# Weights' buffers at the far end of SBUF, every later tile 52 KB lower

## The chip, the cores and the metric

The kernel runs on one core of one Trainium2 chip. The metric is the device time of one execution in microseconds; lower is better. Three runs of the kernel before gave 2146.89, 2148.67 and 2943.94 us; the median, 2148.67 us, is the time before. The profile is of one further execution, which took 2149.47 us.

## The reference

Two decoder layers over a residual stream x of 512 tokens and 1024 channels, in float32. Each layer has three parts: a half-step SwiGLU feed-forward network (FFN) of width 2816, a token mixing of 16 heads in three groups, and a second half-step FFN. Shift, scale and gate of every part come from silu(c) times a matrix.

```python
def swiglu(h, w1, w3, w2):
    return (jax.nn.silu(h @ w1) * (h @ w3)) @ w2
...
        h = modulate(rmsnorm(x, norm_g[layer, 0]), sh1, sc1)
        x = x + 0.5 * g1 * swiglu(h, ffn_w1[layer, 0], ffn_w3[layer, 0], ffn_w2[layer, 0])

        h = modulate(rmsnorm(x, norm_g[layer, 1]), sh2, sc2)
        proj = h @ w_in[layer]
...
        o = jnp.concatenate([oa, ob, oc], axis=2)
        o = (_rms(o).reshape(B, S, D_MIX) * out_g[layer].astype(jnp.float32)).astype(x.dtype)
        x = x + g2 * (o @ w_out[layer])

        h = modulate(rmsnorm(x, norm_g[layer, 2]), sh3, sc3)
        x = x + 0.5 * g3 * swiglu(h, ffn_w1[layer, 1], ffn_w3[layer, 1], ffn_w2[layer, 1])
```

## The kernel before

**Layout of the data.** x lies transposed in SBUF, eight tiles of 128 channels by 512 tokens. All matrices are read from HBM in 338 pieces of at most 128 x 1024 float32 (512 KB), in the order of use. `fetch` (L262) loads a piece into a tile `raw` by a DMA on the SP queue and copies it on ScalarE to `whi` in the type float32r; `load_piece` (L273) lets VectorE write the rest, `wlo` = `raw` - `whi` (L280). Activations are split the same way: normalized x into `hh` and `hl`, the FFN's gated product into `gh` and `gl`.

**The product.** Every large product is done in three matmuls, `mm3` (L302): high by high (L308), high by low (L309), low by high (L310). A matmul on TensorE has a stationary operand (at most 128 x 128, brought in by a weight load that the profile lists as PEld) and a moving operand that streams past it.

- In the first half of an FFN (`h @ w1`, `h @ w3`) a slice of 128 columns of `whi` or `wlo` is stationary and `hh` or `hl` moves, 512 columns at a time.
- In the second half (`@ w2`) a slice of `whi` or `wlo` is stationary and `gh` or `gl` moves, 512 columns; the last two outputs of each FFN are done in halves of 256 columns (`TAIL`, `HALVES`). The first head of the next FFN and the output projection (`out_last`) also move `hh` and `hl` 256 columns at a time.
- In the mixing, `proj_tok` (L542) has it the other way round: `hh` or `hl` is stationary and `whi` or `wlo` moves, 256 or 328 columns. `proj_feat` (L557) has weights stationary and `hh` or `hl` moving, 512 columns, in bursts of 24 matmuls.

TensorE therefore reads two SBUF tiles at a time: the moving one, and the stationary one of the next matmul.

**The order.** Within an engine instructions run in program order. The mixing's order over its parts is written out by hand (`PLAN`, L130). There are three `raw` buffers and five each of `whi` and `wlo`, so that loading, splitting and multiplying overlap: ScalarE's copy of a piece waits until TensorE has done with the piece five before.

**Where the tiles lie.** Each pool is a stretch of every partition; pools are laid one behind the other in the order in which they are opened in `Net.__init__` and later, and tiles keep fixed addresses. Counting the tiles' sizes gives this map (bytes from the start of a partition; the last column is the address modulo 512, the size of a row of 128 float32 numbers):

| pool and tile | address | modulo 512 |
|---|---|---|
| `consts`: x and the small tables; `rmat` at 19,520 | 1,152 to 24,128 | 64 (`rmat`) |
| `weights`: 3 `raw`, 5 `whi`, 5 `wlo`, 4 KB each, 53,248 bytes in all | 24,128 to 77,376 | 64 |
| `acts`: 8 `hh`, 8 `hl`, 2 KB each | 77,376 to 110,144 | 64 |
| `tiny` | 110,144 to 113,600 | mixed |
| `fp` (open in the FFNs): `gh` and `gl` among them, 2 KB each | 125,888 to 195,520 | 448 |
| `mp` (open in the mixing): `qk`, `v`, `att` among them | 113,600 to 229,056 | 64 (these three) |

The FFNs' pool `fp` and the mixing's pool `mp` take turns in the stretch above 113,600.

Of the kernel before, what the change touches and what calls it, by code (L numbers as in the profile page):

```python
# [182 lines left out]
class Net:  # L183
    def __init__(self, tc, ctx, io):
        self.tc, self.nc, self.ctx, self.io = tc, tc.nc, ctx, io
        self.n = 0
        self.cp = ctx.enter_context(tc.tile_pool(name="consts", bufs=1))
        self.wp = ctx.enter_context(tc.tile_pool(name="weights", bufs=1))
        self.hp = ctx.enter_context(tc.tile_pool(name="acts", bufs=1))
        self.sp = ctx.enter_context(tc.tile_pool(name="tiny", bufs=1))  # L190
        pp = ctx.enter_context(tc.tile_pool(name="psum", bufs=1, space=PSUM))
        self.bank = lambda tag, shape: self.t(pp, tag, shape, bufs=2)
        self.new_z = lambda: self.t(pp, "z", [P, 1024], bufs=3)
        self.xs = self.cp.tile([P, KC, S], F32, name="xs")
        self.x = [self.xs[:, k, :] for k in range(KC)]
        self.piece, self.fetched = -1, None
        self.queue, self.delayed = [], []
        self.order = ExitStack()
# [951 lines left out]
```

## Time and profile before

| | |
|---|---|
| median of the three runs | 2148.67 us |
| the profiled execution | 2149.47 us |
| its span, first to last instruction | 2147.7 us |
| mean granted TensorE clock | 0.996 |
| busy: TensorE matmul / weight load / VectorE / ScalarE | 2094.9 / 1806.0 / 1305.2 / 831.2 us |
| read from HBM | 256.55 MB |

[...] In a view by stretches the count in brackets holds every instruction that runs at any time in the stretch, so also the ones still running at its left edge.

### The profile page before, as it was taken

To read this page: it belongs to the slowest core of one execution; us is meant where nothing else is said; L and a number is where in the kernel's file an instruction comes from. 1 tells how busy PE (TensorE), PEld (TensorE's weight loads), DVE (VectorE), ACT (ScalarE), POOL (GpSimd) and SP (SyncE) were. 2 spreads that over 40 slices of the span, in tenths; PEclk is the share of its full clock that TensorE was granted. 3 is DMA by queue.
4 is the path that set the end of the run, shared out by engine and by line. 5 is a ranking of instruction groups with operands and counts; after the bars stand their busy time and mean duration, and the time that the engine had idled before them with its cause. 6 is when DMAs were issued, how large, how long until landed. Compare 5 with 4: busy or idle time off the path is not lost.

```text
span 2147.7 us, 28762 instructions
## 1 busy us (share of the span) xinstructions
PE 2094.9 (98%) x11280; PEld 1806.0 (84%) x11280; DVE 1305.2 (61%) x2607; ACT 831.2 (39%) x1295; POOL 2.9 (0%) x12
## 2 busy tenths in 40 slices
PE   6999999999999999999999999999999999999999
PEld 5888888888998888888898888888889988888888
DVE  8772753679989777375364333346899886333332
ACT  3321222467664432122242222324766644222220
POOL 0000000000000000000000000000000000000000
PEclk9999999999999999999999999999999999999999
DMA  8783752342333378376334333324333223323331
GB/s 296 265 283 98 264 172 90 102 106 63 101 93 90 120 264 283 99 264 199 96 99 137 98 95 94 96 85 122 90 86 103 71 74 108 97 89 98 99 101 56
DMA packets 86151, 281.75 MB, mean 131 GB/s; under 512 B 10752, under 2 KB 13312, under 8 KB 86016
## 3 DMA queue, kind: packets, MB, share of 16 engines
q1 hardware_dynamic: 84576, 277.83, 41.5%
q8 instruction: 88, 1.44, 0.3%
q10 hardware_dynamic: 1440, 2.10, 0.3%
q14 instruction: 47, 0.39, 0.1%
HBM read 256.55 MB, written 2.10 MB: 120 GB/s over the span
## 4 chain that ended last, share of the span: by engine, by line
PE 82%; DVE 12%; ACT 2%; DMA 2%; issue 1%; SPq 0%; ACTq 0%; DVEq 0%
PE z L308 23%; PE z L310 23%; PE z L309 23%; PE b L308 3%; PE b L310 3%; PE b L309 3%; DVE att L568 2%; DVE sc L855 2%; DVE wlo L280 2%; DVE m L854 1%; PE z L613 1%; DMA qk<-qk 1%; PE z L657 1%; PE z L706 1%; DVE tf L718 1%
## 5 line engine op out<-in xcount | busy, mean ns | idle before, releaser
L280 DVE TENSOR_TENSOR wlo<-raw,whi 128x1024 fp32r<-128x1024 f32 (+1 forms) x338 | 412.2, 1220 | 537.4 <-ACT whi L270 535.2
L270 ACT CAST whi<-raw 128x1024 fp32r<-128x1024 f32 (+1 forms) x338 | 354.3, 1049 | 864.0 <-PE z L309 793.0
L308 PE MATMUL z<-hh,whi 128*128 128x512 f32 (+1 forms) x1616 | 597.1, 370 | 6.7 <-DVE xs L987 3.9
L310 PE MATMUL z<-hh,wlo 128*128 128x512 f32 (+1 forms) x1616 | 595.6, 369 | 1.9 <-DVE wlo L280 1.9
L309 PE MATMUL z<-hl,whi 128*128 128x512 f32 (+1 forms) x1616 | 596.8, 370 | 0.5
L308 PEld LDWEIGHTS z<-hh,whi 128*128 128x128 f32 x1616 | 305.7, 189 | 58.7 <-DVE xs L987 4.3
L310 PEld LDWEIGHTS z<-hh,wlo 128*128 128x128 f32 x1616 | 305.3, 189 | 53.2 <-DVE wlo L280 2.6
L309 PEld LDWEIGHTS z<-hl,whi 128*128 128x128 f32 x1616 | 305.7, 189 | 52.2 <-DVE hl L430 1.3
L308 PE MATMUL z<-gh,whi 128*128 128x512 f32 (+1 forms) x792 | 293.6, 371 | 0.0
L309 PE MATMUL z<-gl,whi 128*128 128x512 f32 (+1 forms) x792 | 292.7, 370 | 0.0
L310 PE MATMUL z<-gh,wlo 128*128 128x512 f32 (+1 forms) x792 | 289.3, 370 | 0.0
L349 DVE CUSTOM_DVE_ANT_0 adaw<-adaw,silc 128x1024 f32<-128x1024 f32 x144 | 171.0, 1221 | 26.2 <-DMA adaw<-in_w_ada_dram 26.1
L308 PEld LDWEIGHTS z<-gh,whi 128*128 128x128 f32 x792 | 148.9, 188 | 29.7
L310 PEld LDWEIGHTS z<-gh,wlo 128*128 128x128 f32 x792 | 148.9, 188 | 27.8
L309 PEld LDWEIGHTS z<-gl,whi 128*128 128x128 f32 x792 | 149.0, 188 | 26.6
L308 PE MATMUL b<-whi,hh 128*128 128x256 f32 x544 | 157.8, 290 | 4.1 <-DVE v L647 3.6
L310 PE MATMUL b<-whi,hl 128*128 128x256 f32 x544 | 155.7, 286 | 0.0
L309 PE MATMUL b<-wlo,hh 128*128 128x256 f32 x544 | 155.6, 286 | 0.0
L506 DVE SCALAR_TENSOR_TENSOR xs<-z,mod,xs 128x512 f32<-128x512 f32 (+1 forms) x72 | 49.7, 691 | 124.6 <-PE z L310 124.5
L308 PEld LDWEIGHTS b<-whi,hh 128*128 128x128 f32 x544 | 105.7, 194 | 5.1 <-issue 4.0
L309 PEld LDWEIGHTS b<-wlo,hh 128*128 128x128 f32 x544 | 105.7, 194 | 0.2
L310 PEld LDWEIGHTS b<-whi,hl 128*128 128x128 f32 x544 | 105.6, 194 | 0.0
(144 smaller groups left out, 2260.1 us busy)
## 6 DMA issues: line engine op xcount, KB each, us to landing
raw<-in_w_dram SPq DMA_DIRECT2D x332, 512.0 KB, 3.6
adaw<-in_w_ada_dram SPq DMA_DIRECT2D x144, 512.0 KB, 4.7
qk<-qk SPq DMA_DIRECT2D x144, 128.0 KB, 2.3
qk<-qk SPq DMA_DIRECT2D x24, 96.0 KB, 3.2
xs<-in_x_dram SPq DMA_DIRECT2D x4, 512.0 KB, 5.3
raw<-in_w_dram SPq DMA_DIRECT2D x4, 492.0 KB, 3.5
silc<-in_c_dram SPq DMA_DIRECT2D x3, 512.0 KB, 5.0
out_dram<-xs ACTq DMA_DIRECT2D x6, 256.0 KB, 2.0
```

The costliest lines, as they stand in the source:

```text
L270: nc.scalar.copy(hi[:, :n], raw[:, :n])
L280: self.nc.vector.tensor_sub(lo[:, :n], raw[:, :n], hi.bitcast(F32)[:, :n])
L308: mm(out, l[0], r[0], start=start, stop=False, **kw)
L309: mm(out, l[0], r[1], start=False, stop=False, **kw)
L310: mm(out, l[1], r[0], start=False, stop=stop, **kw)
L349: r = self.nc.vector.tensor_tensor_reduce(w, w, self.silc, 1.0, 0.0, op0=ALU.mult, op1=ALU.add, accum_out=m[:, j:j + 1])
L506: nc.vector.scalar_tensor_tensor(self.x[m][:, cs], ps[:, cs], gate[:, m:m + 1], self.x[m][:, cs], op0=ALU.mult, op1=ALU.add)
L568: nc.vector.tensor_sub(unit_sbuf(lo, u), src, unit_sbuf(hi.bitcast(F32), u))
L613: self.nc.tensor.matmul(out, a, b, start=start and i == 0, stop=stop and i == 1, skip_group_check=True)
L657: nc.tensor.matmul(outs[e][:, HT - w:], lhs, a[:, o:o + w], start=i + j == 0, stop=c == KEY_UNITS[u][-1][1] and j == 1, skip_group_check=True)
L706: mm = lambda out, l, r: nc.tensor.matmul(out, l, r, start=False, stop=True, skip_group_check=True)
L855: nc.vector.match_replace(sc, m8, sc, TAKEN)
```

## The change

The pool `weights` is opened with `side="right"`: its 53,248 bytes are taken from the far end of the partition in place of the near one. The allocator's far end is at byte 229,344, so the pool now begins at 176,096, which is 480 modulo 512 (it was 64). Every pool opened later (`acts`, `tiny`, `fp`, `mp`) begins 53,248 bytes lower: `acts` at 24,128, `fp` and `mp` at 60,352. As 53,248 is 104 times 512, the addresses of their tiles modulo 512 stay what they were: 64 for `hh` and `hl`, 448 for `gh` and `gl`. `consts` stays. No instruction is added, removed or moved, and the buffers are as many and as large as before.

```diff
         self.cp = ctx.enter_context(tc.tile_pool(name="consts", bufs=1))
-        self.wp = ctx.enter_context(tc.tile_pool(name="weights", bufs=1))
+        self.wp = ctx.enter_context(tc.tile_pool(name="weights", bufs=1, side="right"))
         self.hp = ctx.enter_context(tc.tile_pool(name="acts", bufs=1))
         self.sp = ctx.enter_context(tc.tile_pool(name="tiny", bufs=1))
```

## The prediction

> **What bounds the kernel.** I read the head of the page first, then the chain of work that ended last, then the groups of instructions with shapes kept apart.
>
> ```profile
> span 2147.7 us, 28762 instructions
> PE 2094.9 (98%) x11280; PEld 1806.0 (84%) x11280; DVE 1305.2 (61%) x2607; ACT 831.2 (39%) x1295; POOL 2.9 (0%) x12
> ...
> PE 82%; DVE 12%; ACT 2%; DMA 2%; issue 1%; SPq 0%; ACTq 0%; DVEq 0%
> ```
>
> TensorE is busy for 98% of the span and carries 82% of the chain. No instruction changes, so the time can only move if instructions take another time at other addresses. The first question is whether the trace of before shows any such dependence. It does. These are TensorE's largest groups, all of one shape and type, 512 moving columns against a slice of `whi` or `wlo`:
>
> ```profile
> L309 PE MATMUL z<-hl,whi 128*128 128x512 f32 x1296 | 505.4, 390 | 0.0
> L310 PE MATMUL z<-hh,wlo 128*128 128x512 f32 x1296 | 505.1, 390 | 0.0
> L308 PE MATMUL z<-hh,whi 128*128 128x512 f32 x1296 | 505.1, 390 | 2.8 <-ACT hh L429 2.8
> ...
> L308 PE MATMUL z<-gh,whi 128*128 128x512 f32 x616 | 243.6, 396 | 0.0
> L309 PE MATMUL z<-gl,whi 128*128 128x512 f32 x616 | 243.2, 395 | 0.0
> L310 PE MATMUL z<-gh,wlo 128*128 128x512 f32 x616 | 240.3, 395 | 0.0
> ```
>
> With `hh` or `hl` moving one lasts 390 ns, with `gh` or `gl` 395 to 396 ns. Durations overlap, so the pace comes from stretches without a gap: two with 512 columns, then two with 256, with the first and the last matmul that each counts.
>
> ```profile
> 210.00:320.00 110.00, 110.00 (x487) 1.00 0.65 215
> 842.00:892.00 50.00, 50.00 (x216) 1.00 0.47 156
> 1096.00:1107.00 11.00, 11.00 (x94) 1.00 0.27 79
> 2130.00:2144.00 14.00, 14.00 (x120) 1.00 0.13 47
> ```
>
> ```profile
> 209.63 0.39 PE L308 MATMUL z<-hh,whi 128*128 128x512 f32 x1
> 319.79 0.39 PE L308 MATMUL z<-hh,whi 128*128 128x512 f32 x1
> 841.80 0.40 PE L308 MATMUL z<-gh,whi 128*128 128x512 f32 x1
> 891.86 0.39 PE L310 MATMUL z<-gh,wlo 128*128 128x512 f32 x1
> 1095.79 0.28 PE L308 MATMUL z<-hh,whi 128*128 128x256 f32 x1
> 1106.95 0.28 PE L308 MATMUL z<-hh,whi 128*128 128x256 f32 x1
> 2129.82 0.28 PE L308 MATMUL z<-gh,whi 128*128 128x256 f32 x1
> 2143.93 0.28 PE L310 MATMUL z<-gh,wlo 128*128 128x256 f32 x1
> ```
>
> With `hh` and `hl`: 110.16 us over 486 intervals, 226.7 ns. With `gh` and `gl`: 50.06 over 215, 232.8 ns. The granted clock is 1.00 in both, and neither stretch has a gap. At 256 columns it is the other way round: 11.16 over 93 is 120.0 ns with `hh`, 14.11 over 119 is 118.6 ns with `gh`. So there are two paces, a regular one (226.7 and 120.0) and a ragged one (232.8 and 118.6). DMA traffic does not tell them apart: the slower stretch of 512 columns has the lighter load (0.47 against 0.65). A burst in the mixing shows `hh` itself at the ragged pace and then settling:
>
> ```profile
> 470.71 0.40 PE L308 MATMUL b<-hh,whi 128*128 128x512 f32 x1
> 470.94 0.39 PE L309 MATMUL b<-hl,whi 128*128 128x512 f32 x1
> 471.18 0.39 PE L310 MATMUL b<-hh,wlo 128*128 128x512 f32 x1
> ...
> 472.08 0.39 PE L308 MATMUL b<-hh,whi 128*128 128x512 f32 x1
> ...
> 472.99 0.39 PE L309 MATMUL b<-hl,whi 128*128 128x512 f32 x1
> ```
>
> From 470.71 to 471.18 two intervals take 470 ns, 235 each; from 472.08 to 472.99 four take 910, 227.5 each. Same tiles, same clock. I read this as a phase: a run of matmuls either falls into step after a few, or, with `gh` and `gl`, never does. What differs between the tiles that fall into step and those that do not is where the moving one lies relative to the stationary one. `hh` and `whi` have the same address modulo 512 (64 and 64) and lie in the same half of the partition; `gh` and `whi` have neither (448 against 64, and mostly over 114,688 against under 77,376).
>
> **The change part by part.** *First, `hh` and `hl` against weights.* After the change they lose both: 64 against 480 modulo 512, near end against far end. If either relation is what lets them fall into step, they take the ragged pace, 232.8 - 226.7 = 6.1 ns more. That concerns 3 x 1296 = 3888 matmuls in the FFNs, which run back to back and set the end: 3888 x 6.1 ns = +23.7 us. No row shows this pair of addresses. From above I bound the price by the ragged intervals in the burst, 235 - 226.7 = 8.3 ns, which makes +32.3 us. From below it is a gain, down to the bare stream of columns. A stretch at half the granted clock shows that:
>
> ```profile
> 459.23:460.90 1.67, 1.67 (x6) 0.50 0.38 88
> ...
> 459.23 0.63 PE L310 MATMUL b<-hh,wlo 128*128 128x512 f32 x1
> 459.66 0.63 PE L613 MATMUL z<-qk,qk 128*128 128x512 f32 x1
> ```
>
> One interval takes 430 ns at a clock of 0.50; halved, an estimate for the full clock is 215 ns, 11.7 ns below the pace of now: 3888 x -11.7 ns = -45.5 us. I take 6.1, since the nearest row is a moving tile of the same width against the same weights that differs in just these relations.
>
> *The same tiles in short bursts and halves.*
>
> ```profile
> L308 PE MATMUL b<-whi,hh 128*128 128x256 f32 x544 | 157.8, 290 | 4.1 <-DVE v L647 3.6 <-DVE osb L693 0.4
> L308 PE MATMUL z<-hh,whi 128*128 128x256 f32 x320 | 92.0, 289 | 3.9 <-DVE xs L987 3.9
> L308 PE MATMUL b<-hh,whi 128*128 128x512 f32 x208 | 83.6, 403 | 1.2 <-DVE qk L579 1.2
> L308 PE MATMUL z<-gh,whi 128*128 128x256 f32 x176 | 50.0, 284 | 0.0
> ```
>
> The bursts of 512 columns (3 x 208 = 624) already spend about half their time at the ragged pace: 624 x 3 ns = +1.9 us (0 to 3.8). The 3 x 320 = 960 halves would gain 1.4 ns each, -1.3 us. Of the mixing's 3 x 544 = 1632 with weights moving I count half of 1.4 ns, since there TensorE also waits for others: -1.2 us (0 to -2.3).
>
> *Second, `gh` and `gl`.* 448 against 480 is still unequal, and `gh` now lies near while the weights lie far: I leave them at the ragged pace, 0. If they fell into step it would be 3 x 616 x -6.1 ns = -11.3 us, and +0.7 us for their 3 x 176 halves.
>
> *Third, VectorE, ScalarE and the DMA.* Weights are split at the near end and the modulation's products are made at the far end, with the same number of elements:
>
> ```profile
> L280 DVE TENSOR_TENSOR wlo<-raw,whi 128x1024 fp32r<-128x1024 f32 x332 | 405.8, 1223 | 527.5 <-ACT whi L270 525.4
> L349 DVE CUSTOM_DVE_ANT_0 adaw<-adaw,silc 128x1024 f32<-128x1024 f32 x144 | 171.0, 1221 | 26.2 <-DMA adaw<-in_w_ada_dram 26.1
> raw<-in_w_dram SPq DMA_DIRECT2D x332, 512.0 KB, 3.6
> adaw<-in_w_ada_dram SPq DMA_DIRECT2D x144, 512.0 KB, 4.7
> ```
>
> 1223 against 1221 ns: VectorE does not mind where the data lies, and I put ScalarE at the same 0. The far tile's DMA lands in 4.7 us against 3.6; it is issued in pairs, which may be all of it. If the far end were the cause, `raw` would land 1.1 us later. Three buffers hide that except where the chain runs through a load, twice in the list of its longest pieces:
>
> ```profile
> 711.64 3.45 DMA raw<-in_w_dram
> 1772.20 3.55 DMA raw<-in_w_dram
> ```
>
> That is 0 to +2.2 us, and I take 0.
>
> The sum is 23.7 + 1.9 - 1.3 - 1.2 = +23.1 us on the profiled execution's 2149.47 us (span 2147.7 and 1.8 around it): 2172.6. That execution stands 0.8 us over the median, so the forecast is 2171.8, say 2172 us, 1.1% slower.
>
> [...]
>
> **The rivals.** (1) *Nothing moves.* The pace follows from the moving tile alone: its own address modulo 512 (64 regular, 448 ragged), which the change leaves alone, or something else in the FFN's second half. For it: every ragged long run is `gh` and `gl`, whose residue is unlike all others. Against it: `hh` is ragged at 470.71 with the same address. Time: 2148.7, between 2146 and 2151. (2) *Faster, the other side.* It is the distance of the moving tile from the near end that makes it ragged, so `gh` and `gl`, at 72,640 to 142,272 after, come into step and `hh` stays so: -11.3 + 0.7 = -10.6 us, 2138. It decides if at least half of the 1848 matmuls take 227 ns. (3) *Both trade places*, since -32 modulo 512 happens to suit `gh`: 23.1 - 10.6 = +12.5, 2161. (4) *All products of 512 columns run at the bare stream*: 2148.7 - 45.5 = 2103.2. No row shows it at the full clock. (5) *The new residue is worse than any seen*: to pass 2% takes 43 us, 11 ns on each of 3888, above the 8.3 ns of the burst.
>
> **How the numbers follow.** The forecast has 0.40, nothing moves 0.31, faster by 10.6 us 0.12, trading places 0.10, beyond 2% slower 0.05, the bare stream 0.02. The range runs from rival 2, 2138, to the upper price of the first term, 2149.5 + 32.3 less 0.8, 2181, and leaves out 0.07 and the outer edges of the others. The forecast's own range is 2164 to 2181. A measurement of this kernel can tell about 2% from no change: faster by over 2% is rival 4, 0.02; slower by over 2% rival 5, 0.05; within 2% all else, 0.93.
>
> **What the changed profile would show.** If the first step is right, the group `z<-hh,whi` at 512 columns lasts 395 or more, and a stretch of 110 us in the FFN's first half counts some 474 matmuls where it counted 487. If 487 again, the step is wrong. `z<-gh,whi` at 390 would mean rival 2 or 3. VectorE's split at 1223 ns and `raw` landing at 3.6 us test the third part. The prediction is wrong if the two paces have nothing to do with the pair of addresses.

## The result, and the profile after

The changed kernel takes 2174.07 us (median of 4 runs, 2173.35 to 2176.14) against 2148.15 us for the kernel before in the same series, an increase of 25.9 us. Without the one slow execution of the kernel before (2943.94 us) it is 1.0125 times as long, 95% interval 1.0113 to 1.0137. It is slower, by 1.2%, and the forecast of 2172 us was 2 us off.

The order of instructions is the same on every engine. The head of the page after, and the line of the chain by engine:

```profile
span 2171.5 us, 28762 instructions
...
PE 2121.4 (98%) x11280; PEld 1803.3 (83%) x11280; DVE 1305.0 (60%) x2607; ACT 830.9 (38%) x1295; POOL 3.6 (0%) x12
...
PE 82%; DVE 13%; ACT 2%; DMA 2%; issue 1%; SPq 0%; ACTq 0%; DVEq 0%
```

The span has grown by 23.8 us, TensorE's busy time by 26.5, VectorE's and ScalarE's not at all. The groups with shapes kept apart (count, then busy time in us and mean ns of one, then idle time before) say which matmuls:

```profile
L309 PE MATMUL z<-hl,whi 128*128 128x512 f32 x1296 | 515.6, 398 | 0.0
L310 PE MATMUL z<-hh,wlo 128*128 128x512 f32 x1296 | 511.7, 395 | 0.0
L308 PE MATMUL z<-hh,whi 128*128 128x512 f32 x1296 | 510.3, 394 | 2.8 <-ACT hh L429 2.8
L280 DVE TENSOR_TENSOR wlo<-raw,whi 128x1024 fp32r<-128x1024 f32 x332 | 406.0, 1224 | 553.6 <-ACT whi L270 551.7
L270 ACT CAST whi<-raw 128x1024 fp32r<-128x1024 f32 x332 | 348.4, 1050 | 880.4 <-PE z L309 806.9 <-PE b L309 29.7 <-DMA raw<-in_w_dram 15.5
L308 PE MATMUL z<-gh,whi 128*128 128x512 f32 x616 | 244.0, 396 | 0.0
L309 PE MATMUL z<-gl,whi 128*128 128x512 f32 x616 | 243.6, 395 | 0.0
L310 PE MATMUL z<-gh,wlo 128*128 128x512 f32 x616 | 240.7, 396 | 0.0
```

With `hh` and `hl` moving a matmul of 512 columns lasted 390 ns and now lasts 394 to 398, as long as with `gh` and `gl`, which have not changed. For the pace, the same two kinds of stretch as in the prediction, with the first and the last matmul that the first one counts:

```profile
210.00:320.00 110.00, 110.00 (x473) 1.00 0.67 215
850.00:900.00 50.00, 50.00 (x216) 1.00 0.48 153
```

```profile
209.75 0.39 PE L308 MATMUL z<-hh,whi 128*128 128x512 f32 x1
319.88 0.40 PE L309 MATMUL z<-hl,whi 128*128 128x512 f32 x1
```

110.13 us over 472 intervals is 233.3 ns, where it was 226.7; the count fell from 487 to 473. With `gh` and `gl` the count in 50 us is 216 as before. 6.6 ns on 3 x 1296 matmuls are 25.7 us, about the whole difference of the medians, 25.9. The two spans differ by only 23.8, but that is no sign of something given back: the profiled execution of before, 2149.47 us, lies above the others at its pace (2146.89 to 2148.67), and the one of after, 2173.35, is the fastest of its four.

The loads were untouched. The DMA issues of weights and of the modulation's rows, with KB each and the median us from issue to landing:

```profile
raw<-in_w_dram SPq DMA_DIRECT2D x332, 512.0 KB, 3.6
adaw<-in_w_ada_dram SPq DMA_DIRECT2D x144, 512.0 KB, 4.7
```

3.6 and 4.7 us, as before, though `raw` now lies at the far end and `adaw` 52 KB lower.

### The profile page after: what moved, and what is told of

It is laid out like the page before. It is cut to its first block, busy times and chain, and to the rows that moved or that the text cites. A ratio compares the mean times of both kernels' runs of the same rounds, so it can differ in the third digit from the quotient of the medians.

```text
span 2171.5 us, 28762 instructions
## 1 busy us (share of the span) xinstructions
PE 2121.4 (98%) x11280; PEld 1803.3 (83%) x11280; DVE 1305.0 (60%) x2607; ACT 830.9 (38%) x1295; POOL 3.6 (0%) x12
## 4 chain that ended last, share of the span: by engine, by line
PE 82%; DVE 13%; ACT 2%; DMA 2%; issue 1%; SPq 0%; ACTq 0%; DVEq 0%
PE z L309 24%; PE z L308 23%; PE z L310 23%; PE b L308 2%; PE b L309 2%; PE b L310 2%; DVE att L568 2%; DVE sc L855 2%; DVE m L854 2%; DVE wlo L280 1%; PE z L613 1%; DMA qk<-qk 1%; PE z L657 1%; DVE tf L718 1%; DVE osb L666 1%
## 5 line engine op out<-in xcount | busy, mean ns | idle before, releaser
L309 PE MATMUL z<-hl,whi 128*128 128x512 f32 (+1 forms) x1616 | 607.7, 376 | 0.5
L310 PE MATMUL z<-hh,wlo 128*128 128x512 f32 (+1 forms) x1616 | 602.5, 373 | 1.3 <-DVE wlo L280 1.3
```

The lines of the kernel that those rows point to most:

```text
L309: mm(out, l[0], r[1], start=False, stop=False, **kw)
L310: mm(out, l[1], r[0], start=False, stop=stop, **kw)
```

## The experiments

The prediction left two relations open, since the change broke both at once: equal addresses of the moving and the stationary tile modulo some power of two (call it the residue theory), and both tiles in the same half of the partition (the distance theory). A third was rival 1, that the moving tile's own address decides. Gaps of unused bytes ahead of pools tell them apart. In every kernel below the instructions and their order are those of the kernel before. Where 512 bytes of the scratch at the near end are given up, it is for room: only 288 bytes were free.

### Four gaps

**e1_fp128** puts `gh` and `gl` at the weights' residue, and leaves them as far away as they were. The gap shifts every tile of the FFNs' pool by 128 bytes, not these two alone.

```diff
         self.fp = es.enter_context(self.tc.tile_pool(name=self.name("fp"), bufs=1))
+        self.fp.tile([P, 32], F32, name=self.name("gap"))
```

> Kernel before with a gap of 128 bytes ahead of the FFNs' tiles: gh and gl then lie at 64 modulo 512, as whi, wlo, hh and hl do; nothing else moves, and gh stays far from the weights. Residue theory (a run falls into step when the moving and the stationary tile have equal addresses modulo some power of two up to 512): gh at 512 columns comes to 226.7 ns from start to start, about 10.6 us faster than before, 2138 us. Distance theory (both tiles must lie in the same half of the partition): gh stays at 232.8 ns, 2148 us. Theory of the moving tile alone (its own residue must be 64): 2138 us as well.

**e2_all288** moves weights and activations together, still near.

```diff
+        ctx.enter_context(tc.tile_pool(name="gap", bufs=1)).tile([P, 72], F32, name="gap")
         self.wp = ctx.enter_context(tc.tile_pool(name="weights", bufs=1))
```

> Kernel before with a gap of 288 bytes ahead of the weights: all weights and activations move up together, to 352 modulo 512 (gh and gl to 224); weights stay near, differences between tiles are kept. Residue theory: as before, 2148 us, hh at 226.7 ns. Distance theory: 2148 us. Theory of the moving tile alone: hh at 352 is out of step, 233 ns, about 2172 us.

**e3_acts288** puts the same gap between the weights and the activations.

```diff
         self.wp = ctx.enter_context(tc.tile_pool(name="weights", bufs=1))
+        ctx.enter_context(tc.tile_pool(name="gap", bufs=1)).tile([P, 72], F32, name="gap")
         self.hp = ctx.enter_context(tc.tile_pool(name="acts", bufs=1))
```

> Kernel before with the gap of 288 bytes behind the weights: weights stay near and at 64, hh and hl go to 352 modulo 512, still right behind them. Residue theory: hh falls out of step, 230 to 237 ns, 2165 to 2190 us, around 2172. Distance theory: nothing changes, 2148 us. Theory of the moving tile alone: about 2172 us.

**e4_far64** is the changed kernel with its weights lowered by 416 bytes.

```diff
+        ctx.enter_context(tc.tile_pool(name="gap", bufs=1, side="right")).tile([P, 104], F32, name="gap")
         self.wp = ctx.enter_context(tc.tile_pool(name="weights", bufs=1, side="right"))
...
-    return bacc.Bacc("TRN2", target_bir_lowering=False, num_devices=1, dynamic_dma_scratch_size=1024)
+    return bacc.Bacc("TRN2", target_bir_lowering=False, num_devices=1, dynamic_dma_scratch_size=512)
```

> Changed kernel with a gap of 416 bytes at the far end, so that the weights stay far but lie at 64 modulo 512 as hh and hl do (the scratch at the near end is 512 bytes smaller, which makes room and lowers consts and activations by 512). Residue theory: hh at 226.7 ns again, 2148 us. Distance theory: as the changed kernel, 2174 us. Theory of the moving tile alone: hh was at 64 in the changed kernel too, so 2174 us.

| run | us (median) | against the kernel before, 95% interval | residue | distance | moving tile alone |
|---|---|---|---|---|---|
| e1_fp128 | 2136.3 | 0.9949 (0.9934 to 0.9964) | 2138 | 2148 | 2138 |
| e2_all288 | 2147.41 | 1.0002 (0.9993 to 1.0012) | 2148 | 2148 | 2172 |
| e3_acts288 | 2173.11 | 1.0119 (1.0104 to 1.0134) | 2172 | 2148 | 2172 |
| e4_far64 | 2146.59 | 0.9998 (0.9989 to 1.0008) | 2148 | 2174 | 2174 |

Only the residue theory has all four. Four rows carry the verdict, all from the groups by shape. In e1_fp128, `gh` far from the weights at an equal residue:

```profile
L308 PE MATMUL z<-gh,whi 128*128 128x512 f32 x616 | 240.7, 391 | 0.0
```

In e2_all288, `hh` at another address of its own, 352, and equal to the weights:

```profile
L309 PE MATMUL z<-hh,whi 128*128 128x512 f32 x1296 | 504.7, 390 | 2.8 <-ACT hh L430 2.8
```

In e3_acts288, `hh` right behind the weights at an unequal one:

```profile
L309 PE MATMUL z<-hh,whi 128*128 128x512 f32 x1296 | 512.5, 396 | 2.8 <-ACT hh L430 2.8
```

And in e4_far64, `hh` far from the weights at an equal one:

```profile
L309 PE MATMUL z<-hh,whi 128*128 128x512 f32 x1296 | 504.6, 390 | 2.8 <-ACT hh L430 2.8
```

391 ns in e1_fp128 where it was 396, and 396 in e3_acts288 where it was 390; e2_all288 and e4_far64 keep the 390 of the kernel before. In e2_all288 both tiles also move by 288 bytes against everything that stays where it was, so in these runs it is their relation to each other that counts. The kernel e1_fp128 is also the fastest so far: 10 us under the kernel before, for 128 unused bytes.

### Which differences are in step

The next two kernels give `gh` and `gl` another residue in each of three stretches of the run, by gaps of 96, 64 and 48 numbers (**e5_scan_a**) and 16, 80 and 40 (**e6_scan_b**) ahead of the FFNs' tiles; the first entry, 32, belongs to the start, which has no `gh`.

```diff
         self.n = 0
+        self.gaps = [32, 96, 64, 48]
...
         self.fp = es.enter_context(self.tc.tile_pool(name=self.name("fp"), bufs=1))
+        self.gaps, gap = self.gaps[1:], self.gaps[0]
+        self.fp.tile([P, gap], F32, name=self.name("gap"))
```

> Kernel before with gaps of different size ahead of the FFNs' tiles, so that gh and gl lie 256 bytes (first FFN), 128 bytes (second and third) and 64 bytes (fourth) past the weights' address modulo 512. A difference of 384, ragged in the kernel before, rules out that equality modulo 128 or 64 is enough. If equality modulo 256 is enough, the first FFN's second half runs at 226.7 ns and the others at 230 to 237; if it takes equality modulo 512, all three are ragged, 230 to 237 ns, and the whole takes 2145 to 2156 us.

> The same with differences of 448 (first FFN), 192 (second and third) and 32 bytes (fourth). If the pace depends on equality alone, all three run at 230 to 237 ns, as 384 did. If a small difference costs little, 32 bytes runs at 227 to 229 ns and 192 at 233.

They took 2143.15 and 2146.34 us in one run each, beside 2146.06 for the kernel before. What matters is the count of matmuls in stretches that hold `gh` and `gl` alone; a pace follows as (length + 0.39 us) / count, good to about 1 ns. First e5_scan_a, with differences of 256, 128 and 64 bytes:

```profile
143.00:193.00 50.00, 50.00 (x222) 1.00 0.49 159
838.00:888.00 50.00, 50.00 (x217) 1.00 0.49 158
1900.00:1945.00 45.00, 45.00 (x198) 1.00 0.31 94
```

Then e6_scan_b, with 448, 192 and 32:

```profile
143.00:193.00 50.00, 50.00 (x216) 1.00 0.50 158
838.00:888.00 50.00, 50.00 (x216) 1.00 0.50 158
1900.00:1945.00 45.00, 45.00 (x194) 1.00 0.31 94
```

256 bytes apart is in step (227.0 ns); 128 is not (232.2), 448 and 192 are not (both 233.3), 32 is not (234.0). 64 lies between, 229.2 ns. So among these differences it takes equality modulo 256, which e5_scan_a's expectation had as one of its two cases. The mild case of e6_scan_b, that a small difference costs little, is out: 32 bytes costs as much as any, within the 1 ns of this count, and 64 the least. With what the other kernels hold, at 512 columns, every multiple of 32 has been seen:

| moving minus stationary, modulo 256 | seen in | pace or duration |
|---|---|---|
| 0 | `hh` before; e4_far64, e5_scan_a | 226.7 to 227.0 ns |
| 32 | e6_scan_b; `hh` in e3_acts288 | 234.0; 396 ns long |
| 64 | e5_scan_a | 229.2 |
| 96 | `hh` after | 233.3 |
| 128 | `gh` before; e5_scan_a | 232.8; 232.2 |
| 160 | `gh` and `gl` in e3_acts288 | 396 to 397 ns long |
| 192 | e6_scan_b, twice | 233.3 |
| 224 | `gh` after | 233.3 |

### One tile in three

What does a matmul pay for: its own pair, or a disturbed neighbour? In **e7_lo128** `wlo` alone is 128 bytes off, in **e8_hl128** `hl` alone; a second gap behind keeps the addresses of all later tiles, and both give up 512 bytes of the scratch.

```diff
         self.fetched = None
+        if self.piece == 0:
+            self.wp.tile([P, 32], F32, name="gap_lo")
         lo = self.t(self.wp, "wlo", [P, 1024], F32R, bufs=5)
```

In e8_hl128 the gap stands between the first `hh` and the first `hl`:

```diff
-            self.h.append(tuple(self.t(self.hp, tag, [P, S], F32R, bufs=8) for tag in ("hh", "hl")))
+            hh = self.t(self.hp, "hh", [P, S], F32R, bufs=8)
+            if not self.h and not hasattr(self, "gap_hl"):
+                self.gap_hl = self.hp.tile([P, 32], F32, name="gap_hl")
+            self.h.append((hh, self.t(self.hp, "hl", [P, S], F32R, bufs=8)))
```

> Kernel before with wlo alone 128 bytes on, at 192 modulo 512; whi, hh and hl keep 64 (scratch 512 bytes smaller to make room). One matmul in three then has an unequal pair. If each matmul pays for its own pair, hh at 512 columns runs at (2 x 226.7 + 233) / 3 = 228.8 ns and the whole gets 3888 x 2.1 ns = 8 us slower, 2155 us. If one unequal pair in three keeps the run from falling into step at all, 233 ns and about 2172 us. If nothing hangs on wlo, 2147 us.

> Kernel before with hl alone 128 bytes on, at 192 modulo 512; hh, whi and wlo keep 64 (scratch 512 bytes smaller to make room). Again one matmul in three has an unequal pair, the second (hl against whi, while wlo is loaded). If a matmul pays for its own moving tile against the weights alone, the second lasts 232 to 234 ns from start to start and the first and third 227. If a step in address from one matmul to the next breaks the rhythm, as the run with wlo moved may be read, the second and the third are both slow, 232 to 235 ns, and the whole takes about 2160 us.

e7_lo128 took 2160.44 us, 1.0062 times the kernel before (1.0045 to 1.0079): 13 to 14 us more, between the 8 and the 25 that were expected of its two theories, so neither has it. Its groups:

```profile
L313 PE MATMUL z<-hh,wlo 128*128 128x512 f32 x1296 | 515.2, 398 | 0.0
L312 PE MATMUL z<-hl,whi 128*128 128x512 f32 x1296 | 514.0, 397 | 0.0
L311 PE MATMUL z<-hh,whi 128*128 128x512 f32 x1296 | 505.1, 390 | 2.8 <-ACT hh L432 2.8
```

Two in three are slow: the one that uses `wlo` (398 ns), and the one before it (397), whose own pair is equal but during which `wlo` is loaded:

```profile
211.45 0.40 PE L312 MATMUL z<-hl,whi 128*128 128x512 f32 x1
211.45 0.19 PEld L313 LDWEIGHTS z<-hh,wlo 128*128 128x128 f32 x1
```

The third, 390, is undisturbed. The starts in the trace say the same: from one matmul to the next it takes 226.8 ns behind L311, 232.4 behind L312 and 234.1 behind L313, on average over the FFNs.

e8_hl128 took 2162.81 us in one run, beside 2147.31. In it the pace depends on the stretch. Four stretches that hold `hh` and `hl` alone, one in the first FFN, two in the third and one in the fourth:

```profile
210.00:320.00 110.00, 110.00 (x482) 1.00 0.67 216
1115.00:1210.00 95.00, 95.00 (x409) 1.00 0.40 125
1280.00:1390.00 110.00, 110.00 (x482) 1.00 0.33 99
1815.00:1910.00 95.00, 95.00 (x413) 1.00 0.32 99
```

By (length + 0.39 us) / count that is 229.0, 233.2, 229.0 and 231.0 ns, with the same tiles at the same addresses and the same clock. So the addresses do not fix the pace by themselves: one set of them ran at 229.0, 231.0 and 233.2 ns. What picks one of the three, no run shows. The first expectation (only the second matmul slow, 228.8 ns on average by the sum for e7_lo128) fits the stretches at 229.0: there it takes 234 ns behind `hl` and 226 to 227 behind the other two. It does not fit the stretch at 233.2, where all three are slow (236, 234 and 230 ns). The second expectation's total of 2160 is near the time of the run, but its pattern, the second and the third slow, is in none of the stretches. Neither mechanism is settled.

### Far, and in step

**e9_far_equal** leaves the changed kernel's weights where they are and brings the activations to them, 256 bytes apart modulo 512.

```diff
         self.wp = ctx.enter_context(tc.tile_pool(name="weights", bufs=1, side="right"))
+        ctx.enter_context(tc.tile_pool(name="gap", bufs=1)).tile([P, 40], F32, name="gap")
         self.hp = ctx.enter_context(tc.tile_pool(name="acts", bufs=1))
...
         self.fp = es.enter_context(self.tc.tile_pool(name=self.name("fp"), bufs=1))
+        self.fp.tile([P, 32], F32, name=self.name("gap"))
```

> Changed kernel, weights at the far end and at 480 modulo 512, with a gap of 160 bytes ahead of the activations and one of 128 bytes ahead of the FFNs' tiles, so that hh, hl, gh and gl all lie at 224, equal to the weights modulo 256. If equality modulo 256 is what counts and distance is nothing, both halves of the FFNs run at 226.7 ns and the whole takes 2136 us, as with the first gap kernel. If equality modulo 512 is needed, hh stays ragged and it takes 2172 us. If the far end costs by itself, it lies over 2140 us.

It took 2136.72 us, 0.9953 times the kernel before (0.9935 to 0.9971). Two of its groups:

```profile
L309 PE MATMUL z<-hh,whi 128*128 128x512 f32 x1296 | 504.6, 390 | 2.8 <-ACT hh L430 2.8
...
L309 PE MATMUL z<-gh,whi 128*128 128x512 f32 x616 | 240.4, 390 | 0.0
```

Both kinds are at 390 ns with the weights at the far end. The far end shows no cost, 2136.72 us against 2136.3 in e1_fp128, where the weights are near; the change's whole loss, and the 10 us that the kernel before was already losing, went with 288 unused bytes.

## Why the prediction was right

**The first term** was the forecast: `hh` and `hl` fall out of step, 6.1 ns on 3888 matmuls, +23.7 us. It measured 6.6 ns and 25.7 us, inside the bounds and 2.0 over the term. The price was taken from `gh` and `gl`, ragged in the kernel before, and that row was the right neighbour: unequal differences other than 64 cost 5.5 to 7.3 ns in the stretches counted in the table above. At a difference of 64 the cost was 2.5 ns (229.2 in e5_scan_a against 226.7), so some luck was in it that the far end left 96.

**The relation** was left open between two readings, residue and distance, and both gave the same sum, so the time alone could not have told them apart. e1_fp128, e3_acts288, e4_far64 and e9_far_equal each decide for the residue. The prediction counted it modulo 512; e5_scan_a (227.0 ns at a difference of 256) and e9_far_equal (390 ns at the same difference) show that equality modulo 256 is enough. The sum is the same either way, as 64 against 480 is unequal modulo both.

**The small terms** were 1.9 us for bursts, -1.3 for halves and -1.2 for the mixing, -0.6 together. The times do not resolve them: the kernel's own executions lie further apart than that. Nor do the durations at 256 columns, which for `z<-hh,whi` are 289 ns before, 291 after, and 287 to 292 among kernels that all have `hh` in step (e1_fp128 and e2_all288). The starts in the two traces do. Where the next matmul of the kind follows without a gap, the bursts went from 232.0 to 236.0 ns, +4.0 where 3 was forecast: 624 x 4.0 = +2.5 us. The mixing's matmuls with weights moving went from 119.7 to 118.2 ns, the gain of about 1.4 that was forecast: up to -2.4 us, if all 1632 were on the path. The halves gained nothing. The first line is a stretch of them after the change, the second the same stretch in e3_acts288, at a difference of 32:

```profile
1107.00:1118.00 11.00, 11.00 (x94) 1.00 0.27 72
1107.00:1118.00 11.00, 11.00 (x96) 1.00 0.29 80
```

By (length + 0.28 us) / count that is 120.0 ns after, as before, and 117.5 in e3_acts288, to about 1 ns. So the step from `gh`'s 118.6 ns to `hh` was not sound: at 256 columns what an unequal address gains hangs on the difference, 1.4 ns at 128, nothing at 96, 2.5 at 32. The three terms measure about +0.2 us in place of -0.6, and that two of them nearly cancel was luck.

**`gh` and `gl`** were put at 0 because 448 against 480 is unequal as well. They measured 396, 395 and 396 ns, against 396, 395 and 395, and the count in 50 us stayed at 216.

**VectorE, ScalarE and DMA** were put at 0. The split measured 1224 ns against 1223, ScalarE's copy 1050 against 1051, the landing 3.6 us both times.

**The rivals.** Rival 1, nothing moves, had a chance of 0.31. It rested on the moving tile alone, by its own address or by something else in the FFN's second half. The first form fell with e2_all288, where `hh` at another address of its own stays in step; the second with e1_fp128, where `gh` in the second half comes into step. In the stretches counted above TensorE's pace goes with how two tiles lie to each other: 226.7 ns (before) and 227.0 (e5_scan_a) at equal addresses modulo 256, 229.2 to 234.0 ns at unequal ones, at a granted clock of 1.00. Rival 2, distance from the near end, and rival 3 would have shown `gh` at 390 ns in the changed kernel, where it is 396. Rival 4, the bare stream, estimated at 215 ns, shows in no kernel here, and rival 5 needed 11 ns where 6.6 were measured.

What stays open is the mechanism; no run here looks into it. What they show, at 512 columns, is this. Where the address at which the moving tile begins and that at which the stationary one begins agreed modulo 256, the stretches in the table ran at 226.7 to 227.0 ns, and at 229.2 to 234.0 where they did not. A matmul under which a weight load at a disagreeing address ran was slow although its own pair agreed (e7_lo128: 232.4 ns to the next start, where it was 226.8 behind the undisturbed one). And one set of addresses ran at 229.0 to 233.2 ns (e8_hl128).

## What to carry to other kernels

Where TensorE runs without a gap, read its pace from the starts of matmuls, group by group; two groups of one shape at two paces and one clock, here 226.7 and 232.8 ns at 1.00, are a question about addresses. With 512 moving columns of float32r and a weight load for each matmul, try equal addresses modulo 256 bytes for the moving tiles and the weights (226.7 ns here, against 229.2 to 234.0); at 256 columns equality gained nothing here (120.0 ns, against 117.5 to 120.0). In the kernel before, the 3,456 bytes of `tiny` in between had left `gh` and `gl` unequal unnoticed, and a gap of 32 numbers mended it (e1_fp128: 391 ns for `z<-gh,whi` where it was 396). Here that was worth 10 us of 2147 in the kernel before and cost 26 when the change broke it, with no instruction touched.

## What the runs showed of the hardware

- The pace of TensorE for 512 columns of float32r at a granted clock of 1.00 went with the difference of two SBUF addresses modulo 256: 226.7 ns at 0 (before; 227.0 in e5_scan_a), 229.2 at 64 (e5_scan_a), 232.2 to 234.0 at 32, 128, 192 (e6_scan_b, e5_scan_a), 96 and 224 (after). At 160 the duration was 396 to 397 ns (e3_acts288), where it was 390 at 0 (before).
- At 256 columns the pace was 120.0 ns at a difference of 0 (before) and of 96 (after), 118.6 at 128 (before) and 117.5 at 32 (e3_acts288).
- The same matmuls at the same addresses ran at three mean paces in one execution, 229, 231 and 233 ns (e8_hl128).
- Where a tile lies along the partition made no difference that shows: with the weights' buffers near (before) and far (after) VectorE's split took 1223 and 1224 ns and the DMA landed in 3.6 us; `z<-hh,whi` at equal addresses took 390 ns with the weights near (before) and far (e4_far64).
